# An output projection's loads moved three chunks ahead, and four stored columns turned into four stored rows

## The chip, the cores and the metric

The kernel runs on one core of a Trainium2 chip, as a single launch. The metric is the device time of one execution in microseconds. Engines are named as the profile does: PE is TensorE's matmul and PEld its weight loads, DVE is VectorE, ACT is ScalarE, POOL is GpSimd, and SP is the engine from which most DMAs are issued. A letter q behind an engine (SPq, ACTq) means its sequencer, which issues DMAs.

## The reference

One encoder layer on x of 2048 tokens by 1024 columns, float32. One input projection feeds two groups of heads: gated linear attention (four heads, result `o_a`, 512 columns) and multi-head latent attention (four heads, dense softmax over all 2048 keys, result `o_b`, 512 columns). Both are gated, joined, projected and normalized:

```python
o_a = gla_branch(g_q, g_k, g_v, g_gate, g_lr_f, g_lr_b, ...)
o_b = mla_branch(m_cq, m_ckv, m_kr, m_gate, positions, ...)   # p = softmax(s); o = (p @ v) * silu(gate)
mixed = jnp.concatenate([o_a, o_b], axis=-1) @ w_out
x = layer_norm(DEEPNORM_ALPHA * x + mixed, ln_g, ln_b)
```

The change lies in the last line but one and the last: the output projection with its residual and normalization, and in the softmax's denominators of the last attention block, which that projection reads.

## The kernel before

**Precision.** Every large product is made of three: an operand is split into a high and a low part (`hi`, a ScalarE copy, L336; `lo`, a subtraction on GpSimd or VectorE, L342), and `mm3` (L368 to L370) adds high x high, high x low and low x high.

**Stages.** Two sweeps over the tokens make the projections and the linear attention (to about 670 us in the profile). Then latent attention runs 16 blocks, each one head by 512 queries, with an order of all engines that is written out by hand as places in time (`PLACE`, `PLACE_LAST`, `PLACE_OUT`). Block i = 4b + h covers head h of the 512 tokens b. For each block the unnormalized output, 128 rows by 512 tokens, goes to the DRAM scratch `ob_s[b]` (`yc`, L1428), and the reciprocals of the softmax's sums go to `r_s[b]` (`keep`, L1406). The sums of a block are transposed and reduced into `rc`, a tile of 128 partitions by 4 (`tsum`, `rcp`): token e*128 + p stands in partition p, column e. So `keep` writes 4-byte elements, issued from ScalarE's queue: for blocks 0 to 14 one DMA of all four columns, for the last block one column at a time, after chunks 6, 7, 8 and 9 of the output projection.

**The output projection** (`OutProj`) works on 16 chunks of 128 tokens. Per chunk c:

- `load(c)` (L1589): four DMAs of 256 KB each on SP: `of<-oa_s` (linear attention's part), `gr<-gm_s` (the gate), `gr<-r_s` (the reciprocals, spread over 128 partitions) and `of<-ob_s` (latent attention's part). The tile `of` has two buffers in turn, and from chunk 4 on so has `gr`.
- `split(c)` (L1515): `oh` of the first half on ScalarE, `ol` of it on GpSimd, two multiplications of the second half by gate and reciprocals on GpSimd (L1609), then `oh` and `ol` of the second half.
- `load_res(c)` (L1619): 512 KB of x on SP into `xr`, three buffers.
- `product(c)` (L1640): two column halves of 24 matmuls each on TensorE. Odd chunks put both into a PSUM pair `po`; even chunks use the single banks `pmb` and `px`.
- `residual(c)` (L1651): `rr` = alpha * `xr` + product and its statistics on VectorE. `rr` has three buffers, so that of chunk c is that of chunk c−3, whose store must have landed.
- `finish(c)` (L1660): `u` from the statistics, `Ln` and `Exp` on ScalarE (L381, L382), the rest of the normalization on VectorE (L387 to L390, L1669, L1672), and two stores `out_dram<-rr` on SP (L1673). In the text, ln(c) means its two ScalarE instructions and out(c) its two stores.

Chunks 0 to 3 are woven into the end of the attention's order (`first`). From there on (L1506) the order of ScalarE, GpSimd and SP alone is held to the program's (`LATE_ORDER`), while TensorE and VectorE are ordered by the framework. Each of these queues works strictly in its order. Before the loop the program has load(4), the residual loads of 2 and 3, load(5), finish(0) and finish(1), split(4), the residual load of 4, and residual and finish of 2 and 3. Then, for each c from 4:

```python
with fixed():
    load(c + 2)
    split(c + 1)
    if c + 1 < NCH:
        op.load_res(rest[c + 1])
    op.product(rest[c])
    op.finish(rest[c])
with self.after(*last.values()), fixed():
    for f in {4: (tot, oh, ol), 5: (tsum, rcp), 7: (y, yc)}.get(c, ()):
        f(nb - 1)
    if 6 <= c < 10:
        keep(nb - 1, c - 6)
```

So on SP load(c+2) stands behind out(c−1). Chunks 12 to 15 read `r_s[3]` and `ob_s[3]`, to which the last block's results go in this loop.

Of the kernel before, what the change touches and what calls it, by code (L numbers as in the profile page):

```python
# [9 lines left out]
F32 = mybir.dt.float32  # L10
F32R = mybir.dt.float32r
I32 = mybir.dt.int32
AF = mybir.ActivationFunctionType
# [5 lines left out]
P = 128  # L19
# [8 lines left out]
QB = 512  # L28
# [36 lines left out]
    tot=11.2,  # L65
    tsum=12.04,
    rcp=13.55,
    keep=14.21,
    oh=12.34,
    ol=12.99,  # L70
    y=16.55,
    yc=16.9,
# [255 lines left out]
class K:  # L328
# [380 lines left out]
    def store(self, c):  # L709


        return self.nc.gpsimd if c in STORE_POOL else self.nc.sync
# [546 lines left out]
    def attention(self):  # L1259
        tc, nc = self.tc, self.nc  # L1260
        mm = nc.tensor.matmul
        V, G, Ac = nc.vector, nc.gpsimd, nc.scalar
        NP = NKT // 2
        with ExitStack() as ctx:
            qp = self.wz
            sp = ctx.enter_context(tc.tile_pool(name="sp", bufs=NP + 4, reuse_waits="tile"))
            bp = ctx.enter_context(tc.tile_pool(name="bp", bufs=2, reuse_waits="tile"))
            bank = lambda n, bufs=1: ctx.enter_context(tc.tile_pool(name=n, bufs=bufs, space=PSUM, reuse_waits="tile"))
            pM, pO, pX, pA, pS = bank("pM"), bank("pO"), bank("pX"), bank("pA"), bank("pS", 2)
            blocks = [(h, b) for b in range(NQB) for h in range(H)]  # L1270
            nb = len(blocks)
            stt = [dict(s=[None] * NP) for _ in blocks]
# [130 lines left out]
                V.reciprocal(rc, rc)  # L1403
                d["rc"] = rc

            def keep(i, e=None):  # L1406
                h, b = blocks[i]
                es = slice(0, 4) if e is None else slice(e, e + 1)
                Ac.dma_start(self.r_s[b][:, h].rearrange("o (e p) -> p (o e)", p=P)[:, es], stt[i]["rc"][:, es])

            def oh(i):
                d = stt[i]
# [30 lines left out]
            op = OutProj(self, ctx, qp, bp, sp, pS, pM, pX)  # L1443
# [8 lines left out]
            def at(f, i, j=None):  # L1452
                p = PLACE_LAST.get(f, PLACE[f]) if i == nb - 1 else PLACE[f]
                return p[j] if isinstance(p, tuple) else p

            own = (("tot", tot), ("tsum", tsum), ("rcp", rcp), ("keep", keep), ("oh", oh), ("ol", ol), ("y", y), ("yc", yc))
            for i in range(nb):
                for j in range(NP):
                    t = NP * i + j
# [48 lines left out]
            rest = {c: o for c, o in enumerate(first)}  # L1508

            def load(c):  # L1510
                if c < NCH:
                    rest[c] = dict(c=c)
                    op.load(rest[c])

            def split(c):  # L1515
                if c < NCH:
                    op.hi(rest[c], 0)
                    op.lo(rest[c], 0)
                    op.gate(rest[c])
                    op.hi(rest[c], 1)  # L1520
                    op.lo(rest[c], 1)

            with fixed():
                load(4)
                for c in (2, 3):
                    op.load_res(rest[c])
                load(5)
                for c in (0, 1):
                    op.finish(rest[c])
                split(4)  # L1530
                op.load_res(rest[4])
                for c in (2, 3):
                    op.residual(rest[c], 0)
                    op.residual(rest[c], 1)
                    op.finish(rest[c])
            for c in range(4, NCH):
                with fixed():
                    load(c + 2)
                    split(c + 1)
                    if c + 1 < NCH:  # L1540
                        op.load_res(rest[c + 1])
                    op.product(rest[c])
                    op.finish(rest[c])
                with self.after(*last.values()), fixed():
                    for f in {4: (tot, oh, ol), 5: (tsum, rcp), 7: (y, yc)}.get(c, ()):
                        f(nb - 1)
                    if 6 <= c < 10:
                        keep(nb - 1, c - 6)


class OutProj:
# [190 lines left out]
```

## Time and profile before

| | |
|---|---|
| three runs | 1363.34, 1357.39 and 1355.76 us, median 1357.39 |
| the profiled execution | 1363.85 us |
| its span | 1362.1 us, 1.75 of the execution lie around it |

Windows of the profiled execution, in us from the start of its span:

| stretch | what runs | PE busy | granted PE clock | DMA share |
|---|---|---|---|---|
| 0 to 600 | projections, linear attention | 572.84 of 600 | 0.99 | 0.41 |
| 600 to 700 | their end, start of attention | 97.17 of 100 | 1.00 | 0.47 |
| 700 to 1140 | attention blocks | 439.36 of 440 | 1.00 | 0.18 |
| 1140 to 1193.23 | last block, output chunks 0 to 2 among it | 51.42 of 53.23 | 1.00 | 0.38 |
| 1193.23 to 1352.35 | output chunks 3 to 15 | 149.17 of 159.12 | 0.97 | 0.67 |
| 1352.35 to 1362.1 | last residual, normalization, store | 0.14 of 9.75 | 0.61 | 0.14 |

How to read the rows that follow. A row of a timeline has the start in us, the duration, the engine, the line of the kernel, the operation, the tiles it writes and reads, the shapes, and in brackets the engine's idle time before it with what ended it. Where several of one kind follow each other they are one row with their count, and the duration runs from the first's start to the last's end. A row of windows has, for each engine, the busy time and the number of instructions, then the clock granted to TensorE as a share of full speed, the mean busy share of the 16 DMA engines and the GB/s they moved. A row of DMA issues ends with the median us from issue to landing.

### The profile page before, as it was taken

The page shows a single profiled execution, that of the slowest core. Times are in us where ns is not written, and L with a number is a line of the kernel's source. Part 1 is how long each engine was busy: PE and PEld are TensorE (multiplying, and loading weights), DVE is VectorE, ACT ScalarE, POOL GpSimd, SP SyncE. Part 2 cuts the span into 40 slices and gives each one's busy share as a digit, 9 for nine tenths or more (in the row PEclk, how much of TensorE's full clock was granted, in tenths as well). Part 3 has the DMA queues.
Part 4 walks back from the last instruction along what each step waited for, and adds up shares of the span by engine and source line. Part 5 has one row for each costly group of instructions (what it writes and reads, how often), then busy time and mean ns, then how long its engine had stood idle before and what let it go on. Part 6 is the DMA issues. An engine that isn't in the chain of part 4 may idle for free.

```text
span 1362.1 us, 20027 instructions
## 1 busy us (share of the span) xinstructions
PE 1310.1 (96%) x7120; PEld 1142.6 (84%) x7120; DVE 937.3 (69%) x1683; ACT 814.6 (60%) x1338; POOL 807.5 (59%) x509
## 2 busy tenths in 40 slices
PE   6899999999989999999999999999999999999987
PEld 6789898989979999999788888888888887777775
DVE  7747755454684444455788888888888888397576
ACT  6555555645565555665687878878888887311110
POOL 2542323232357666663198888889999998734352
PEclk9999999999999999999999999999999999999988
DMA  7322222313283566654601111121133110467863
GB/s 250 85 63 79 62 78 74 90 51 89 78 284 132 184 203 196 200 186 148 177 1 39 40 39 39 40 63 55 55 85 86 43 35 27 115 203 177 184 177 116
DMA packets 108836, 147.39 MB, mean 108 GB/s; under 512 B 17886, under 2 KB 63326, under 8 KB 108736
## 3 DMA queue, kind: packets, MB, share of 16 engines
q1 hardware_dynamic: 99408, 143.46, 35.6%
q0 software_dynamic: 832, 2.62, 0.5%
q8 instruction: 56, 0.92, 0.3%
q10 hardware_dynamic: 8496, 0.03, 0.3%
q14 instruction: 44, 0.36, 0.1%
HBM read 94.93 MB, written 51.15 MB: 107 GB/s over the span
## 4 chain that ended last, share of the span: by engine, by line
PE 60%; DVE 4%; DMA 3%; POOL 2%; issue 1%; ACT 1%; SPq 0%; DVEq 0%; POOLq 0%; ACTq 0%
PE pS L1293 4%; PE pS L1296 4%; PE pS L1295 4%; PE pS L1297 4%; PE pS L1294 4%; PE o L368 4%; PE o L369 4%; PE o L370 4%; PE pz L368 2%; PE pz L369 2%; PE pz L370 2%; PE ipm L368 2%; PE ipm L370 2%; PE ipm L369 2%; PE po L370 1%; PE po L369 1%
## 5 line engine op out<-in xcount | busy, mean ns | idle before, releaser
L342 POOL TENSOR_TENSOR pl<-s,ph 128x1024 fp32r<-128x1024 f32 x128 | 307.1, 2416 | 67.2 <-ACT ph L336 61.8
L1315 DVE TENSOR_TENSOR rm<-pS,rm 128x512 f32<-128x512 f32 x210 | 144.8, 690 | 44.6 <-ACT s L1302 39.5
L1302 ACT ACTIVATE s<-pS 128x1024 f32<-128x1024 f32 x128 | 131.4, 1027 | 68.1 <-PE pS L1297 66.7
L1339 DVE TENSOR_TENSOR s<-s,mb 128x1024 f32<-128x1024 f32 x128 | 151.2, 1213 | 9.1 <-PE mb L1333 9.0
L336 ACT ACTIVATE ph<-s 128x1024 fp32r<-128x1024 f32 x128 | 135.1, 1057 | 16.7 <-PE o L370 16.1
L1343 ACT ACTIVATE s<-s 128x1024 f32<-128x1024 f32 x128 | 131.4, 1050 | 13.4 <-DVE s L1339 13.3
L368 PE MATMUL ipa<-wah,xah 128*128 128x384 f32 (+1 forms) x384 | 131.1, 341 | 6.7 <-ACT wah L336 6.7
L838 POOL TENSOR_TENSOR Us<-Us,cw 128x512 f32<-128x512 f32 x16 | 18.2, 1139 | 200.7 <-DVE Us L835 171.3
L370 PE MATMUL ipa<-wah,xal 128*128 128x384 f32 (+1 forms) x384 | 126.0, 328 | 0.0
L369 PE MATMUL ipa<-wal,xah 128*128 128x384 f32 (+1 forms) x384 | 125.5, 327 | 0.0
L1293 PE MATMUL pS<-qh,ckvT_h 128*128 128x512 f32 x256 | 103.7, 405 | 0.7 <-ACT s L1343 0.4
L368 PE MATMUL o<-ph,vh 128*128 128x512 f32 x256 | 102.6, 401 | 0.0
L370 PE MATMUL o<-ph,vl 128*128 128x512 f32 x256 | 101.3, 396 | 0.0
L1296 PE MATMUL pS<-rh,krs 128*128 128x512 f32 x256 | 101.2, 395 | 0.0
L369 PE MATMUL o<-pl,vh 128*128 128x512 f32 x256 | 101.1, 395 | 0.0
L1295 PE MATMUL pS<-qh,ckvT_l 128*128 128x512 f32 x256 | 100.8, 394 | 0.0
L1297 PE MATMUL pS<-rl,krs 128*128 128x512 f32 x256 | 100.7, 393 | 0.0
L1294 PE MATMUL pS<-ql,ckvT_h 128*128 128x512 f32 x256 | 100.6, 393 | 0.0
L1366 DVE TENSOR_TENSOR ap<-ap,s 128x512 f32<-128x512 f32 x120 | 83.1, 692 | 7.5 <-ACT s L1343 5.6
L342 POOL TENSOR_TENSOR ol<-of,oh 128x512 fp32r<-128x512 f32 x32 | 43.4, 1356 | 71.6 <-ACT oh L336 71.6
L368 PEld LDWEIGHTS ipa<-wah,xah 128*128 128x128 f32 x384 | 74.2, 193 | 7.2 <-ACT wah L336 6.7
L368 PE MATMUL pz<-xch,wzh 128*128 128x256 f32 x256 | 75.1, 294 | 0.0
(316 smaller groups left out, 3904.9 us busy)
## 6 DMA issues: line engine op xcount, KB each, us to landing
xcf<-xT_dram SPq DMA_DIRECT2D x16, 512.0 KB, 4.2
xr<-x_dram SPq DMA_DIRECT2D x16, 512.0 KB, 6.9
out_dram<-rr SPq DMA_DIRECT2D x32, 256.0 KB, 2.4
xaf<-xT_dram SPq DMA_DIRECT2D x14, 512.0 KB, 4.3
qdb<-qd_s SPq DMA_DIRECT2D x16, 256.0 KB, 4.7
SU<-su_s SPq DMA_DIRECT2D x16, 256.0 KB, 4.7
oib<-oi_s SPq DMA_DIRECT2D x16, 256.0 KB, 4.7
ub<-u_s SPq DMA_DIRECT2D x16, 256.0 KB, 3.8
```

Source lines behind the costliest of these rows:

```text
L336: return nc.scalar.activation(dst, src, AF.Copy).ins
L342: return e.tensor_tensor(dst, src, hi.bitcast(F32), ALU.subtract).ins
L368: mm(out, ah, bh, start=start, stop=False)
L369: mm(out, ah, bl, start=False, stop=False)
L370: mm(out, al, bh, start=False, stop=stop)
L1293: mm(ps[:, e], kh, qh, start=True, stop=False)
L1294: mm(ps[:, e], kh, ql, start=False, stop=False)
L1295: mm(ps[:, e], kl, qh, start=False, stop=False)
L1296: mm(ps[:, e], kr, rh, start=False, stop=False)
L1297: mm(ps[:, e], kr, rl, start=False, stop=True)
L1315: V.tensor_tensor(d["rm"], src[:, e], d["rm"], ALU.max)
L1339: V.tensor_tensor(s, s, d["mb"][:, None, :].to_broadcast([P, 2, QB]), ALU.subtract)
```

## The change

- `keep` stores all four columns again, and only blocks 0 to 14 use it.
- For the last block, after chunk 6, `turn` transposes `rc` on TensorE into the PSUM tile `rt` (128x4 to 4x128) and copies it with ScalarE into `rr15`, four partitions of 128; `store` writes it from SP to `r_s[3]` as four rows of 512 bytes. The four column stores after chunks 6 to 9 go.
- Before the loop, split(4), a new load(6) and the residual load of 4 come ahead of finish(0) and finish(1).
- In the loop, load(c+3) stands behind split(c+1), in place of load(c+2) ahead of it.

```diff
-            def keep(i, e=None):
+            def keep(i):
                 h, b = blocks[i]
-                es = slice(0, 4) if e is None else slice(e, e + 1)
-                Ac.dma_start(self.r_s[b][:, h].rearrange("o (e p) -> p (o e)", p=P)[:, es], stt[i]["rc"][:, es])
+                Ac.dma_start(self.r_s[b][:, h].rearrange("o (e p) -> p (o e)", p=P), stt[i]["rc"])
+
+            def turn(i):
+
+                d = stt[i]
+                t = pA.tile([P, QB], F32, tag="ap", name=f"rt{i}")
+                nc.tensor.transpose(t[0:4, 0:P], d["rc"], self.ident)
+                d["rr"] = bp.tile([4, P], F32, tag="ofl", name=f"rr{i}", bufs=1)
+                Ac.activation(d["rr"], t[0:4, 0:P], AF.Copy)
+
+            def store(i):
+                h, b = blocks[i]
+                nc.sync.dma_start(self.r_s[b][:, h].rearrange("o (e p) -> (o e) p", p=P), stt[i]["rr"])
...
                 load(5)
+                split(4)
+                load(6)
+                op.load_res(rest[4])
                 for c in (0, 1):
                     op.finish(rest[c])
-                split(4)
-                op.load_res(rest[4])
...
             for c in range(4, NCH):
                 with fixed():
-                    load(c + 2)
                     split(c + 1)
+                    load(c + 3)
...
-                    for f in {4: (tot, oh, ol), 5: (tsum, rcp), 7: (y, yc)}.get(c, ()):
+                    for f in {4: (tot, oh, ol), 5: (tsum, rcp), 6: (turn, store), 7: (y, yc)}.get(c, ()):
                         f(nb - 1)
-                    if 6 <= c < 10:
-                        keep(nb - 1, c - 6)
```

## The prediction

> **What bounds the kernel now.** I began with the page, then cut the last stage at the starts of its chunks, then asked which waits stood in the cuts.
>
> ```profile
> span 1362.1 us, 20027 instructions
> PE 1310.1 (96%) x7120; PEld 1142.6 (84%) x7120; DVE 937.3 (69%) x1683; ACT 814.6 (60%) x1338; POOL 807.5 (59%) x509
> ```
>
> TensorE is the bound, so a change that moves no matmul can only win TensorE's idle or half-clocked time. Windows laid along the output product, one per chunk of 48 matmuls (chunks 4, 5, 6, 7, 10, 11 and 14; columns: length, busy time of each engine, granted clock, DMA share, GB/s):
>
> ```profile
> 1204.16:1215.07 10.91, 10.91 (x50) 8.88 (x48) 10.88 (x24) 1.97 (x6) 2.21 (x3) 1.00 0.51 179
> 1215.07:1228.97 13.90, 11.83 (x50) 8.78 (x49) 12.91 (x21) 2.15 (x5) 6.77 (x5) 1.00 0.47 138
> 1229.32:1244.58 15.26, 12.93 (x52) 10.00 (x50) 12.18 (x18) 2.19 (x5) 9.05 (x7) 0.89 0.53 175
> 1244.58:1255.46 10.88, 10.88 (x50) 9.01 (x48) 5.82 (x12) 1.67 (x4) 5.16 (x4) 1.00 1.00 199
> 1277.95:1290.25 12.30, 11.35 (x50) 8.85 (x49) 10.40 (x17) 1.67 (x4) 4.87 (x4) 1.00 0.69 187
> 1290.25:1308.81 18.56, 13.96 (x50) 10.54 (x49) 10.53 (x14) 2.19 (x5) 9.01 (x7) 0.82 0.60 139
> 1330.57:1341.45 10.88, 10.88 (x50) 9.01 (x49) 10.48 (x15) 1.56 (x4) 5.22 (x4) 1.00 0.43 140
> ```
>
> An undisturbed chunk takes 10.88. Over that, chunk 5 loses 3.0, chunk 6 4.4, chunk 10 1.4 and chunk 11 7.7: 16.5 in all. Chunks 12 to 15 lose nothing with loads two ahead. So the change is judged on four chunks.
>
> Chunk 11 waited for ScalarE's second high part, and that for a load; the first row is TensorE's, the second from the chain of waits, then ScalarE's stores of reciprocals (three of four), then the landings of residual inputs `xr` in this stage:
>
> ```profile
> 1297.60 0.79 PE L368 MATMUL po<-woh,oh 128*128 128x512 f32 x1 [4.47 <-ACT oh L336]
> 1283.38 10.76 DMA of<-ob_s
> 1246.90 0.34 ACTq L1409 DMA_DIRECT2D r_s<-rc  x1
> 1259.16 0.34 ACTq L1409 DMA_DIRECT2D r_s<-rc  x1
> 1284.33 0.33 ACTq L1409 DMA_DIRECT2D r_s<-rc  x1
> DMA to landing us min/median/max: 6.0/6.9/17.9
> ```
>
> Bandwidth around these stores (same columns as above):
>
> ```profile
> 1244.00:1252.00 8.00, 8.00 (x37) 6.64 (x36) 6.02 (x13) 1.04 (x3) 2.52 (x2) 1.00 0.79 260
> 1252.00:1259.00 7.00, 7.00 (x32) 5.74 (x32) 3.27 (x7) 0.99 (x4) 2.66 (x3) 1.00 1.11 59
> 1264.00:1271.00 7.00, 7.00 (x33) 5.79 (x32) 0.00 (x0) 0.63 (x1) 3.55 (x3) 1.00 1.14 80
> 1271.00:1276.00 5.00, 5.00 (x24) 4.14 (x23) 4.27 (x9) 1.00 (x3) 0.00 (x0) 1.00 1.12 310
> 1289.00:1296.00 7.00, 4.13 (x19) 3.08 (x17) 0.20 (x1) 0.00 (x0) 1.65 (x2) 1.00 0.75 119
> ```
>
> Some 5 us after each of these stores of 128 elements of 4 bytes, the DMA engines are as busy as ever and move 59, 80, 119 GB/s in place of 260 to 310, for 7 us. The 17.9 is `xr` of chunk 8, caught by two such jams; it made chunk 8's normalization, and so chunk 10's split, late (1.4). Chunk 11's load was caught by the last jam (7.7). So 9.1 of the 16.5 hangs on how the last block's reciprocals are stored.
>
> Chunk 6 has another cause:
>
> ```profile
> 1212.59 9.38 SPq L1673 DMA_DIRECT2D out_dram<-rr  x4
> 1222.06 0.38 SPq L1600 DMA_DIRECT2D of<-oa_s  x1
> 1230.66 2.64 POOL L1609 TENSOR_TENSOR of<-of,gr 128x512 f32<-128x512 f32 x2 [2.92 <-DMA of<-ob_s]
> ```
>
> Its load stood on SP behind the stores of chunks 2 and 3, though its buffer was free since 1207.1 (`ol` of chunk 4, below).
>
> **The change, part by part.** *Row store.* The four jams go: −1.4 −7.7 = −9.1. Added are one transpose, one ScalarE copy of 4x128 and one 2 KB store. No row shows them; the nearest are the transposes `sx`, 0.27 each, and ScalarE's 0.20 (one element a lane) and 0.62 (512 a lane). The copy is in ScalarE's slack behind chunk 6. The transpose is on TensorE's path: 0.1 to 0.3, I take 0.1. The store has until chunk 12's load, three chunks later. Four ScalarE issues (0.34) leave a queue that is idle there.
>
> *Loads in the loop.* load(c+3) now waits on SP for GpSimd's end of split(c+1) instead of VectorE's out(c−1). Behind it on SP stand `xr` of c+1 and out(c). For the odd chunk 7, ended at 1255.46, ScalarE's normalization came 3.4 later:
>
> ```profile
> 1258.61 0.20 ACT L381 ACTIVATE ln_l<-u 128x1 f32<-128x1 f32 x1 [4.49 <-DVE u L1667]
> ```
>
> So, from the end T of product c−1, split(c+1) begins at T+3.5 and takes 6.7 (rows below): it ends near T+10.2. Four load issues take 2.3; `xr` lands 6.9 after its own: T+19.4, ahead of the end of product c+1 at T+21.8. out(c) is due near T+17, with SP free since T+13; who waits for it is the residual of chunk c+3, at T+43. Nothing new is on the path; were the 2.4 of cover for `xr` gone, each us more would cost one. The gain is chunk 6's 4.4; chunks 12 to 15 show that there is no more.
>
> *The start, split(4) and load(6) ahead of finish(0) and finish(1).* ScalarE, GpSimd and SP keep program order here, VectorE's order is rebuilt. Moved ahead are two ScalarE and four GpSimd instructions and, on SP, four load issues (2.3) and one of `xr` (0.6). Rows of ScalarE (ln of chunk 0, `oh` halves of 4, `oh` of 5), GpSimd (gate of 4, `ol` of 4, `ol` of 5) and VectorE (rr of 2 and 3, u of 3), and landings of the loads issued 1191 to 1195:
>
> ```profile
> 1192.87 0.20 ACT L381 ACTIVATE ln_l<-u 128x1 f32<-128x1 f32 x1 [4.01 <-DVE u L1667]
> 1199.92 0.61 ACT L336 ACTIVATE oh<-of 128x512 fp32r<-128x512 f32 x1
> 1204.69 0.63 ACT L336 ACTIVATE oh<-of 128x512 fp32r<-128x512 f32 x1 [4.16 <-POOL of L1609]
> 1214.34 0.62 ACT L336 ACTIVATE oh<-of 128x512 fp32r<-128x512 f32 x1
> 1201.98 2.67 POOL L1609 TENSOR_TENSOR of<-of,gr 128x512 f32<-128x512 f32 x2
> 1205.40 1.68 POOL L342 TENSOR_TENSOR ol<-of,oh 128x512 fp32r<-128x512 f32 x1 [0.74 <-ACT oh L336]
> 1219.79 1.27 POOL L342 TENSOR_TENSOR ol<-of,oh 128x512 fp32r<-128x512 f32 x1 [0.74 <-ACT oh L336]
> 1201.96 0.68 DVE L1657 SCALAR_TENSOR_TENSOR rr<-xr,pmb 128x512 f32<-128x512 f32 x1
> 1209.24 0.68 DVE L1657 SCALAR_TENSOR_TENSOR rr<-xr,po 128x512 f32<-128x512 f32 x1
> 1213.82 0.14 DVE L1667 TENSOR_SCALAR u<-mv 128x1 f32<-128x1 f32 x1
> of<-ob_s SPq DMA_DIRECT2D x1, 256.0 KB, 7.4
> 1226.62 2.03 SPq L1673 DMA_DIRECT2D out_dram<-rr  x2
> DMA to landing us min/median/max: 4.7/5.3/5.8
> ```
>
> Chunk 4's last load, issued at 1192.9, lands at 1200.3. Gate 2.7, `oh` 0.7, `ol` 1.3: split(4) ends at 1205.1, 2.0 earlier. But ln(0) and ln(1) now stand behind its second `oh`: 1203.7 in place of 1192.9. VectorE does rr of chunk 2 at 1201.7, then waits for ln(0), and goes on at 1205.1. Ahead of rr(3) now stand thirteen operations of 512 columns at 0.62 to 0.7 and some small ones: 1214.0 in place of 1209.2. And rr(3) takes the buffer of rr(0), so out(0) must have landed. out(0) now follows load(6) and `xr` of 4 on SP. In the old order such a group began at 1222.06 and the stores behind it (last two rows) landed at 1232.4 and 1233.0, 10.4 and 11.0 after. From 1205.1 that is 1215.5 to 1216.1; I take 1215.6. Then six more operations to u(3), 1219.5, and chunk 5's split starts at 1220.0 in place of 1214.3: **+5.7**, straight onto chunk 5, whose TensorE waits are on that split. Bounds: +4.1 if out(0) lands in time (1214.0 holds), +9.0 if it lands as late as the slowest store in the chain of waits:
>
> ```profile
> 1261.35 10.20 DMA out_dram<-rr
> ```
>
> (issued at 1208.8, landing at 1219.0). Chunk 6's split then has its load early, starts after ln(4) near 1228 and ends by 1236; its product starts at 1235. It needs the second half 2.8 later, so its 4.4 is gone whatever chunk 5 does.
>
> The 5.7 us wait ahead of chunk 5 may bring the clock down, as here (the stretches after chunk 6's and chunk 11's waits):
>
> ```profile
> 1234.97:1238.38 3.41, 3.01 (x7) 2.43 (x8) 3.38 (x7) 0.93 (x3) 2.43 (x3) 0.50 0.51 191
> 1296.41:1303.24 6.83, 5.51 (x12) 3.92 (x13) 6.59 (x12) 1.55 (x4) 4.88 (x5) 0.50 0.65 184
> ```
>
> Half a clock for 3.4 us costs 1.7. But the first twelve matmuls of chunk 5 wait for its second half anyway (6.7 us from the start of the split, 1214.34, to its end, 1221.06), and run inside that wait. I take 0.3, bounds 0 and 1.7. The Trainium skill, "TensorE: Matmul & The Clock Gate", Part 1, says that an idle window of some 3.4 us halves the clock until a busy one has passed; by it the full 1.7 would come, a total of −6.0. The rows agree on the size and are shorter on the cause: 1.71 of waiting was enough at chunk 6.
>
> Sum: −9.1 −4.4 +5.7 +0.3 +0.1 = **−7.4**. The profiled execution took 1363.85 (span 1362.1); with the change 1356.4. The runs shown are 1363.34, 1357.39 and 1355.76, so the profile is at their slow end. Taken off the median of 1357.39: **1350.0**.
>
> **Rivals.**
> 1. *The median run never lost the jams.* Whether chunk 11's load beats the last jam is close: the slow stretch is there at 1289, and a load issued at 1283.38 that took the 6.0 of the quickest `xr` would land at 1289.4. The profile lies 6.5 above the median, near the 7.7. Then the change saves the median run only −4.4 +6.1 −1.4: +0.3, **1357.7**. Against it: the early stages have waits of their own that could make the spread.
> 2. *Slower: the start costs more than chunk 6 gives back.* ln(0) behind split(4) is the mechanism. With out(0) at 1219.0, the clock at 1.7, and no jam losses in the median run: −4.4 +9.0 +1.7 +0.1 = +6.4, **1363.8**. It decides as soon as chunk 5's split starts more than 4.4 after 1214.3 and the jams are no loss. For it: VectorE was busy 10.88 of 10.91 through chunk 4, so it has nothing to absorb a stall with.
> 3. *The row store jams too*, or the jam is not the store's: chunks 10 and 11 keep 9.1, and the sum is +1.7, **1359.1**. Against it: the slow stretches follow three of the four stores. By the Trainium skill, "DMA: Bandwidth & Descriptors", Specifications, transfers under 512 B are read-modify-write; rows of 512 B would be just clear of it. No row here shows such a store.
> 4. *out(0) lands in time and nothing is lost to the clock*: −9.1 −4.4 +4.1 +0.1 = −9.3, **1348.1**.
>
> **How the numbers follow.** The forecast, 1350.0, with its own range 1348 to 1353, holds 0.42; rival 1 0.22, rival 2 0.18, rival 3 0.07, rival 4 0.09, and 0.02 is for what I overlooked. The range 1346 to 1361 leaves out rival 2 and that rest: 2 in 10. A change under 0.5% (6.8 us, about what a measurement of this kernel can tell from none) ends at 1350.6 and 1364.2. Faster: rival 4 and 0.30 of the forecast, 0.39. Slower: two thirds of rival 2, where the landing or the clock costs more than its bounds here, and the rest, 0.14. Same: what is left, 0.47.
>
> **What would show it.** Right: no stretch under 200 GB/s with a DMA share near 1 between chunks 7 and 12; chunks 6 to 15 at 10.9 each; chunk 5 near 19.6 with its first wait on ScalarE's `oh`; ln(0) on ScalarE after chunk 4's second `oh`; rr of chunk 3 waiting for a store `out_dram<-rr`. Wrong: chunk 5 at 14 or less (the start costs nothing), slow stretches that remain, or waits on `xr` in the loop.

## The result, and the profile after

| | runs | median us | lowest and highest |
|---|---|---|---|
| before | 22 | 1357.20 | 1351.04 to 1363.34 |
| after | 22 | 1361.68 | 1357.74 to 1363.75 |

The ratio is 1.003, with a 95% interval of 1.0019 to 1.0041: 4.5 us slower, where 7.4 us faster was forecast. The two profiled executions say the reverse: before took 1363.85, after 1359.89. So two questions are open: which of the steps failed, and why profile and median differ in sign.

The first lines of after's page:

```profile
span 1358.1 us, 20026 instructions
PE 1308.9 (96%) x7121; PEld 1142.0 (84%) x7121; DVE 950.6 (70%) x1683; ACT 813.7 (60%) x1339; POOL 805.7 (59%) x509
```

TensorE is still the bound, and again what counts is its idle time in the output chunks. Windows of after, one for each of chunks 5, 6, 7, 8 and 11 (columns as before: length, then busy time of PE, PEld, DVE, ACT and POOL, granted clock, DMA share, GB/s); chunk 8's begins with `y`, the last block's three matmuls, which take 0.7:

```profile
1215.13:1234.00 18.87, 13.88 (x50) 10.39 (x50) 18.07 (x29) 3.60 (x9) 10.17 (x8) 0.82 0.39 133
1234.35:1245.33 10.98, 10.98 (x51) 8.99 (x50) 8.79 (x15) 1.36 (x4) 4.08 (x4) 1.00 0.60 192
1245.36:1256.24 10.88, 10.88 (x50) 9.01 (x49) 8.31 (x16) 0.57 (x3) 1.30 (x1) 1.00 0.69 228
1256.24:1272.05 15.81, 12.89 (x53) 9.35 (x52) 11.75 (x14) 3.35 (x8) 10.89 (x8) 1.00 0.42 115
1293.81:1304.69 10.88, 10.88 (x49) 9.01 (x48) 10.60 (x15) 1.56 (x4) 5.37 (x5) 1.00 0.65 198
```

Chunk 6's 4.4 is gone and so is chunk 11's 7.7; chunk 5 has grown from 13.90 to 18.87, as the prediction had it (+5.0 for +5.7). Chunk 8 is new: with `y` it needs 11.7 undisturbed (10.9 and 0.7 in before) and took 15.8, 4.1 more. The prediction had chunks 6 to 15 at 10.9 each and no cost at chunk 8.

The slow stretches behind the column stores are gone, too. Windows of after over the times of four rows that the prediction shows of before (slow there at 1252, 1264 and 1289, fast at 1271):

```profile
1252.00:1259.00 7.00, 5.97 (x25) 4.26 (x24) 4.28 (x9) 0.79 (x2) 1.10 (x1) 1.00 0.55 197
1264.00:1271.00 7.00, 6.81 (x30) 5.63 (x31) 4.86 (x6) 0.74 (x2) 5.61 (x5) 1.00 0.76 185
1271.00:1276.00 5.00, 5.00 (x24) 4.14 (x23) 2.66 (x5) 0.00 (x0) 0.00 (x0) 1.00 1.02 330
1289.00:1296.00 7.00, 7.00 (x32) 5.79 (x32) 6.83 (x9) 0.63 (x1) 4.17 (x4) 1.00 0.53 186
```

At shares of 0.53 to 0.76 the DMA engines move 185 to 197 GB/s and at 1.02 they move 330; in before's slow stretches they moved 59 to 119 at shares of 0.75 to 1.14.

ScalarE's timeline in after, at the start and around chunk 8:

```profile
1202.39 0.63 ACT L336 ACTIVATE oh<-of 128x512 fp32r<-128x512 f32 x1 [6.42 <-POOL of L1619]
1202.93 0.18 ACT L381 ACTIVATE ln_l<-u 128x1 f32<-128x1 f32 x1
...
1219.34 0.61 ACT L336 ACTIVATE oh<-of 128x512 fp32r<-128x512 f32 x1
...
1250.80 0.20 ACT L382 ACTIVATE ln_y<-ln_l 128x1 f32<-128x1 f32 x1
1257.04 0.27 ACT L1416 ACTIVATE rr<-rt 4x128 f32<-4x128 f32 x1 [6.04 <-PE y L369]
1257.22 0.61 ACT L336 ACTIVATE oh<-of 128x512 fp32r<-128x512 f32 x1
```

At the start ln(0) stands right behind chunk 4's second `oh`, and chunk 5's split begins at 1219.34 (forecast 1220.0). At chunk 8 the new copy `rr<-rt` stands idle for 6.04 before it runs. Its input `rt` was there since 1245.6, when the transpose between chunks 6 and 7 ended. What ended the wait is `y`, which runs after chunk 7. Behind the copy, in program order, stands the first `oh` of chunk 8. By ScalarE alone it could have run at 1251.0; it ran at 1257.2, and TensorE had to wait for both halves of split(8).

Why should a copy of `rt` wait for `y`? `turn` gives `rr15` the tag `ofl` with one buffer. That is the buffer of `ofl15`, the low part of the last block's output, and `y` reads it. By this the copy may not write before `y` has read. The first two experiments test it.

### The profile page after: what moved, and what is told of

Same layout as the page of the kernel before. It is cut to its first block, busy times and chain, and to the rows that moved or that the text cites. A ratio compares the mean times of both kernels' runs of the same rounds, so it can differ in the third digit from the quotient of the medians.

```text
span 1358.1 us, 20026 instructions
## 1 busy us (share of the span) xinstructions
PE 1308.9 (96%) x7121; PEld 1142.0 (84%) x7121; DVE 950.6 (70%) x1683; ACT 813.7 (60%) x1339; POOL 805.7 (59%) x509
## 4 chain that ended last, share of the span: by engine, by line
PE 46%; issue 4%; POOL 2%; DMA 1%; DVE 1%; ACT 1%; SPq 0%; DVEq 0%; POOLq 0%; ACTq 0%
PE pS L1293 4%; PE pS L1296 4%; PE pS L1295 4%; PE pS L1297 4%; PE pS L1294 4%; PE o L368 4%; PE o L369 4%; PE o L370 4%; PE po L369 1%; PE po L370 1%; PE po L368 1%; POOL of L1619 1%; PE pmb L370 1%; PE pmb L369 1%; DMA of<-oa_s 1%
## 5 line engine op out<-in xcount | busy, mean ns | idle before, releaser
L1315 DVE TENSOR_TENSOR rm<-pS,rm 128x512 f32<-128x512 f32 x210 | 144.9, 690 | 44.5 <-ACT s L1302 39.4
L369 PEld LDWEIGHTS ipa<-wal,xah 128*128 128x128 f32 x384 | 74.0, 193 | 1.3 <-DVE wal L342 0.6
```

Source lines behind the costliest of these rows:

```text
L369: mm(out, ah, bl, start=False, stop=False)
L1315: V.tensor_tensor(d["rm"], src[:, e], d["rm"], ALU.max)
```

## The experiments

All executions lose their time in a few chunks, so one table serves them all. It gives, for each profile, the end of chunk 4, the time lost over the undisturbed 10.88 in chunks 5, 6, 8 (with `y`, over 11.7) and 10 to 12 together, and the stretch from the end of chunk 4 to the end of the span. Without any loss that stretch is about 130.7 (before: 147.0 − 16.5 = 130.5; after: 143.0 − 8.0 − 0.1 − 4.1 = 130.8). Chunks from 7 on that are not listed lose under 0.3.

| kernel, execution us | end of 4 | 5 | 6 | 8 | 10 to 12 | stretch |
|---|---|---|---|---|---|---|
| before, 1363.85 | 1215.1 | 3.0 | 4.4 | 0 | 9.1 | 147.0 |
| before_again, 1369.23 | 1218.3 | 3.1 | 4.6 | 0 | 11.0 | 149.2 |
| before_look2, 1358.81 | 1217.1 | 3.0 | 1.9 | 0 | 4.5 | 139.9 |
| before_look3, 1364.46 | 1217.9 | 3.0 | 4.5 | 0 | 6.7 | 144.7 |
| before_look4, 1365.65 | 1219.0 | 3.0 | 4.8 | 0 | 6.6 | 144.9 |
| before_look5, 1360.88 | 1218.1 | 3.1 | 4.3 | 0 | 3.1 | 141.0 |
| before_look6, 1364.50 | 1218.4 | 3.1 | 4.8 | 0 | 5.6 | 144.3 |
| after, 1359.89 | 1215.1 | 8.0 | 0.1 | 4.1 | 0 | 143.0 |
| after_again, 1362.24 | 1216.9 | 8.6 | 0.1 | 4.0 | 0 | 143.6 |
| after_look3, 1362.33 | 1215.9 | 9.7 | 0.1 | 4.0 | 0 | 144.6 |
| own_buffer, 1359.12 | 1215.7 | 10.7 | 0.1 | 0 | 0 | 141.6 |
| row_alone, 1356.92 | 1219.0 | 2.9 | 2.4 | 0 | 0 | 136.1 |
| row_shared, 1360.90 | 1215.0 | 3.1 | 6.1 | 4.1 | 0 | 144.1 |
| loads_alone, 1366.36 | 1217.2 | 8.8 | 0.1 | 6.8 | 1.2 | 147.4 |
| finish_first, 1354.83 | 1218.8 | 2.8 | 0.7 | 0 | 0 | 134.3 |
| stores_first, 1356.20 | 1217.7 | 5.1 | 0.7 | 0 | 0 | 136.7 |
| split5_early, 1350.93 | 1217.1 | 0 | 1.2 | 0 | 0 | 132.1 |

The times that follow were measured later, on three chips. There before took medians of 1363.0 to 1365.0, where the first pair had 1357.2, so kernels are compared by their ratio to before on the same chip and in the same set of runs.

### A buffer of its own for the copy, and the reverse

own_buffer is the changed kernel with

```diff
-                d["rr"] = bp.tile([4, P], F32, tag="ofl", name=f"rr{i}", bufs=1)
+                d["rr"] = bp.tile([4, P], F32, tag="rr", name=f"rr{i}", bufs=1)
```

> The changed kernel with one edit: rr15 gets a buffer of its own (tag rr) in place of ofl's. Theory W (the copy waits for y because it reuses the buffer that y reads, and split(8) stands behind it on ScalarE): the copy runs at about 1246, right after rt; the first oh of chunk 8 at about 1251 in place of 1257.2; chunk 8 takes 10.9 in place of 14.2 and starts 0.6 sooner; 4.0 less than the changed kernel, about 1357.7. Rival (the copy waits for y by the order of the queues, or chunk 8's split is late for another reason, such as its load): the copy still ends its wait with y, chunk 8 keeps its 14.2, about 1361.7. In both, chunk 5 keeps 18.8 with its wait of 4.7.

row_shared is the row store alone, in the order of before, with the buffer shared as in the changed kernel (row_alone, below, has it with a buffer of its own):

```diff
-                d["rr"] = bp.tile([4, P], F32, tag="rr", name=f"rr{i}", bufs=1)
+                d["rr"] = bp.tile([4, P], F32, tag="ofl", name=f"rr{i}", bufs=1)
```

> row_alone with one edit, the reverse of own_buffer's: rr15 shares ofl's buffer, as in the changed kernel. Theory W: the copy waits for y here too, with loads and start as in the kernel before; chunk 8 takes about 14 in place of 10.9 and the stretch from the end of chunk 4 to the end of the span 140 in place of 136.1. Rival (the wait bites only where the loads stand behind the splits): chunk 8 keeps 10.9.

ScalarE's timeline in own_buffer, then the window of `y` and chunk 8 there, then the same two of row_shared:

```profile
1252.82 0.20 ACT L382 ACTIVATE ln_y<-ln_l 128x1 f32<-128x1 f32 x1
1252.93 0.25 ACT L1416 ACTIVATE rr<-rt 4x128 f32<-4x128 f32 x1
1253.09 0.61 ACT L336 ACTIVATE oh<-of 128x512 fp32r<-128x512 f32 x1
```

```profile
1259.53:1271.27 11.74, 11.74 (x53) 9.66 (x52) 10.43 (x16) 2.04 (x5) 5.98 (x5) 1.00 0.71 232
```

```profile
1258.02 0.27 ACT L1416 ACTIVATE rr<-rt 4x128 f32<-4x128 f32 x1 [9.19 <-PE y L369]
1258.19 0.61 ACT L336 ACTIVATE oh<-of 128x512 fp32r<-128x512 f32 x1
```

```profile
1257.35:1273.05 15.70, 12.78 (x53) 9.26 (x52) 13.04 (x16) 3.35 (x8) 10.88 (x8) 1.00 0.51 162
```

With a buffer of its own the copy has no wait: it starts 0.1 behind the second instruction of ln(6), which stands ahead of it on ScalarE (so not right behind `rt`, as I had expected), 6.7 ahead of `y` (near 1259.7), and split(8) starts 0.16 behind it. Chunk 8 loses nothing. With the shared buffer in the old order the copy waits 9.19 for `y`, and chunk 8 loses its 4.1 again. So the wait is the buffer's, whatever the order of the loads, and costs 4.0 to 4.1 in four profiles out of four. The time of own_buffer itself was 1359.65 against 1364.98 for before (ratio 0.9963, 0.995 to 0.9976); row_shared took 1363.87 against 1363.74 (0.9994, 0.9974 to 1.0014). Two expectations missed in other chunks. In own_buffer's profile chunk 5 lost 10.7, and not 8.0; why is seen below. In row_shared's, chunk 6 lost 6.1, and the stretch came to 144.1 in place of 140; chunk 6 runs ahead of the copy, and why it lost so much there stays open.

### The row store alone, and the loads alone

row_alone is before with `turn` and `store` (own buffer) in place of the four column stores, loads and start untouched:

```diff
-                    for f in {4: (tot, oh, ol), 5: (tsum, rcp), 7: (y, yc)}.get(c, ()):
+                    for f in {4: (tot, oh, ol), 5: (tsum, rcp), 6: (turn, store), 7: (y, yc)}.get(c, ()):
                         f(nb - 1)
-                    if 6 <= c < 10:
-                        keep(nb - 1, c - 6)
```

> The kernel before with the row store alone (turn and store after chunk 6, rr15 in a buffer of its own), loads and start as before. Theory J (a median run of before loses little to the column stores: its 1357.2 leaves 2.5 for them after the 3.0 of chunk 5 and the 4.4 of chunk 6): 0 to 2.5 below the kernel before, about 1355. Rival, my forecast's first term (every run loses 9.1): about 1348. In both, no stretch under 200 GB/s with a DMA share near 1 behind chunk 7, and chunks 10 and 11 at 10.9.

loads_alone is the opposite: the start and the loop of the changed kernel, and the four column stores of before. Against before its loop reads:

```diff
-                    load(c + 2)
                     split(c + 1)
+                    load(c + 3)
```

> The kernel before with the loads and the start of the changed kernel, and the four column stores kept. By my terms corrected by the trace of after: chunk 5 +5.0, chunk 6 -4.4, chunk 8 undisturbed by the copy. If loads three ahead also cover the slow stretches behind the column stores, chunks 10 and 11 come to 10.9: +0.6 less up to 2.5 against before, 1355 to 1358. Rival (the slow stretches still bite, at another chunk, because a store of 128 small elements delays whatever load is then under way): a stall of 3 to 8 remains between chunks 8 and 12, 1360 to 1366.

Windows of row_alone: chunks 10 and 11, then a stretch behind the row store in which the DMA engines are busy:

```profile
1279.96:1290.84 10.88, 10.88 (x49) 9.01 (x48) 10.47 (x15) 1.56 (x4) 5.45 (x5) 1.00 0.32 104
1290.84:1301.72 10.88, 10.88 (x49) 9.01 (x48) 7.20 (x14) 1.67 (x4) 3.90 (x4) 1.00 0.79 260
...
1266.00:1273.00 7.00, 7.00 (x33) 5.79 (x32) 5.83 (x10) 1.56 (x4) 2.46 (x3) 1.00 0.69 224
```

The slow stretches and the losses in chunks 10 to 12 go with the column stores, and with nothing else changed. The ratio to before was 0.9949 (0.9932 to 0.9965), or 1357.26 against 1364.98: −7.7. That is well over the 2.5 that I had left for it, and near my first 9.1. Not all of it need be the store's: chunk 6, ahead of these stores, lost 2.4 in this profile, and 4.3 to 4.8 in six of the seven of before. The Trainium skill, "DMA: Bandwidth & Descriptors", Specifications, has transfers under 512 B as read-modify-write; rows of exactly 512 B, one store of four, show no slow stretch here, which agrees.

The row store differs from the column stores in three ways: it is one DMA in place of four, it is made of longer pieces, and it comes from SP and not from ScalarE's queue. The first alone is not it. Block 14's `keep`, the same in both kernels, is a single DMA of 512 elements; in after it is issued at 1154.85 and lands 9.1 later, and windows ahead of that landing and behind it read:

```profile
1161.00:1163.00 2.00, 2.00 (x10) 1.65 (x9) 1.86 (x3) 1.67 (x2) 2.00 (x2) 1.00 1.04 33
1165.00:1167.00 2.00, 2.00 (x11) 1.60 (x9) 0.66 (x1) 0.00 (x0) 0.00 (x0) 1.00 0.56 178
```

Pieces and queue are not told apart by any run here, and that read-modify-write is what slows the rest is not shown either.

loads_alone took 1366.86 against 1364.98 (ratio 1.0022, 1.0007 to 1.0036). Its rows: a slow stretch of its DMA in windows, `xr` of chunk 7 in a view of that tile, ScalarE's and TensorE's timelines, and the window of `y` and chunk 8:

```profile
1262.00:1267.00 5.00, 3.38 (x15) 2.45 (x14) 1.04 (x2) 0.00 (x0) 0.00 (x0) 1.00 0.93 69
```

```profile
DMA to landing us min/median/max: 12.8/12.8/12.8
```

```profile
1268.91 0.20 ACT L381 ACTIVATE ln_l<-u 128x1 f32<-128x1 f32 x1 [9.13 <-DVE u L1668]
...
1269.25 0.58 ACT L1431 ACTIVATE yc<-y 128x512 f32<-128x512 f32 x1
```

```profile
1269.88 0.80 PE L368 MATMUL px<-woh,oh 128*128 128x512 f32 x1 [4.50 <-ACT yc L1431]
```

```profile
1258.90:1277.48 18.58, 14.08 (x54) 11.10 (x52) 11.06 (x17) 2.67 (x6) 6.92 (x6) 0.82 0.75 146
```

The expectation's rival was that a slow stretch delays whatever load is under way, and so it does; that loads three ahead cover the stretches fails. Where TensorE lost time, in chunks 8 and 11, no split waited for its own load; but `xr` of chunk 7, issued at 1253.0, took 12.8 to land. The residual of chunk 7 began at 1265.96, 6.9 after its product; its normalization came late on ScalarE, behind it in program order stood `yc`, which empties the bank that chunk 8's second half needs, and TensorE waited 4.5 for `yc`. Chunk 11 lost its 1.2 to another `xr`: that of chunk 9 took 13.9 to land, its normalization came late, and split(11) stood behind it on ScalarE. So loading further ahead didn't take the column stores' loss away; it moved it.

### The start: what chunk 5 waits for

The changed kernel's start costs chunk 5 its 8.0 to 9.7. VectorE's timeline at rr of chunk 3, first in own_buffer, then in after_look3:

```profile
1217.97 1.28 DVE L1667 SCALAR_TENSOR_TENSOR rr<-xr,po 128x512 f32<-128x512 f32 x2 [3.38 <-DMA out_dram<-rr]
```

```profile
1217.17 1.28 DVE L1667 SCALAR_TENSOR_TENSOR rr<-xr,po 128x512 f32<-128x512 f32 x2 [2.51 <-DMA out_dram<-rr]
```

It waits for a store, out(0), as forecast. In after itself the row names another releaser:

```profile
1215.11 1.28 DVE L1667 SCALAR_TENSOR_TENSOR rr<-xr,po 128x512 f32<-128x512 f32 x2 [2.23 <-PE px L369]
```

But rr of chunk 3 doesn't read `px`, and the second store of out(0), issued at 1208.1, landed 6.8 later, at 1214.9: rr begins 0.2 behind that landing, as in own_buffer (issued at 1209.8, 8.0, landed at 1217.8). That rr waited for the store here too is inferred from this. What the store's landing moves, chunk 5 pays: rr of chunk 3 began at the end of chunk 4 in after, 0.6 behind it in after_again, 1.3 in after_look3 and 2.3 in own_buffer, and chunk 5 lost 8.0, 8.6, 9.7 and 10.7.

Two edits of own_buffer take the mechanism apart. stores_first leaves split(4) ahead of both finishes, but puts the finishes ahead of load(6):

```diff
                 split(4)
-                load(6)
-                op.load_res(rest[4])
                 for c in (0, 1):
                     op.finish(rest[c])
+                load(6)
+                op.load_res(rest[4])
```

> own_buffer with one edit: finish(0) and finish(1) between split(4) and load(6), so that ln(0) still stands behind split(4) on ScalarE, but out(0) no longer behind load(6) on SP. If the landing of out(0) is what held rr of chunk 3 (it had to wait 3.4 for it in own_buffer), it has no wait now, and chunk 5's wait for its split falls from 7.0 to about 3.5. If ln(0) behind split(4) is the cost by itself, the wait stays at 5 to 7.

finish_first puts finish(0) and finish(1) ahead of split(4) and load(6) (as in own_buffer, rr15 has its own buffer):

```diff
+                for c in (0, 1):
+                    op.finish(rest[c])
                 split(4)
                 load(6)
                 op.load_res(rest[4])
-                for c in (0, 1):
-                    op.finish(rest[c])
```

> own_buffer with one edit: finish(0) and finish(1) again ahead of split(4), load(6) behind split(4), and so ahead of out(2) and out(3) but behind out(0). Theory: out(0) then lands before VectorE comes to rr of chunk 3, chunk 5 is back at about 13.9 and chunk 6 at 10.9; the end of chunk 4 to the end of the span takes 133.5 in place of 141.5, about 8 less than own_buffer and 2.5 less than row_alone. Rival (load(6) ahead of out(2) and out(3) costs in another place what it gives at chunk 6): chunks 5 and 6 together lose 5.3 or more, as in row_alone.

Windows of stores_first (TensorE's wait ahead of chunk 5, chunk 5 itself) and of finish_first (chunks 5 and 6):

```profile
1217.89:1219.77 1.88, 0.00 (x0) 0.00 (x0) 1.84 (x5) 0.93 (x3) 0.00 (x0) 1.00 0.62 142
1219.77:1233.74 13.97, 13.20 (x48) 10.08 (x49) 13.59 (x21) 2.04 (x5) 7.87 (x7) 0.88 0.68 227
```

```profile
1218.79:1232.44 13.65, 11.75 (x50) 8.73 (x48) 13.34 (x20) 2.15 (x6) 8.76 (x7) 1.00 0.59 189
1232.79:1244.35 11.56, 11.29 (x52) 8.92 (x50) 9.29 (x17) 1.32 (x5) 5.55 (x4) 1.00 0.61 193
```

Of own_buffer's 10.7 in chunk 5, 5.6 go when out(0) no longer follows load(6) on SP (the wait ahead of the chunk falls from 7.0 to 1.9, further than the 3.5 expected), 2.3 more when ln(0) no longer follows split(4) on ScalarE, and 2.8 were there before. These are differences of single profiles, and own_buffer's 10.7 is the largest of five with this start; against after's 8.0 the first is 2.9. In finish_first load(6) is early all the same, and chunk 6 loses only 0.7. It came to 0.9921 of before (0.9908 to 0.9935), stores_first to 0.9920 (0.9903 to 0.9937); the profiles differ by 2.4 in the stretch, the times don't tell the two apart.

### A version that beats both

split5_early is finish_first with split(5) moved ahead of the residual of chunk 3; in the loop they are then left out for c = 4:

```diff
                     op.finish(rest[c])
+                    if c == 2:
+                        split(5)
+                        load(7)
+                        op.load_res(rest[5])
```

> finish_first with one edit: split(5), load(7) and the residual load of 5 between finish(2) and the residual of chunk 3, where they stood behind finish(3). If chunk 5's loss of 3.0 in the kernel before is only its split standing behind ln(3) on ScalarE, chunk 5 comes to about 11 and the stretch from the end of chunk 4 to the end of the span to 130.6, 3 less than finish_first. Rival (VectorE, which is busy all through chunk 4, or out(3) behind load(7), makes chunk 6 or 7 late by as much): the same as finish_first.

Its windows for chunks 5 and 6:

```profile
1217.10:1227.99 10.89, 10.89 (x50) 8.96 (x49) 10.58 (x24) 1.82 (x6) 2.19 (x3) 1.00 0.73 253
1228.34:1240.44 12.10, 11.28 (x51) 8.91 (x50) 11.93 (x18) 2.19 (x5) 7.32 (x6) 1.00 0.52 177
```

Chunk 5 has no loss left, chunk 6 1.2. The stretch is 132.1, 2.2 less than in finish_first and not 3, since chunk 6 lost 0.5 more. The time is 1350.70 against 1364.96 for before and 1364.87 for the changed kernel on the same chip: 0.9885 of before (0.9872 to 0.9899).

### Before and after again

> The kernel before, unedited, for a second profile. Theory J: chunk 11 loses much less than 7.7 here, since whether its load beats the last slow stretch is a matter of a microsecond; the span is 4 to 8 below 1362.1 by that alone. Rival: chunk 11 loses 7.7 again, and the spread of the times comes from stages ahead of chunk 3, which then ends at another time than 1204.2.

> The changed kernel, unedited, on one chip with the next three. Theory W: chunk 8 loses 4 again behind the copy that waits for y; chunk 5 loses 8 or more behind out(0). On a chip where the kernel before loses 8 to 11 to the slow stretches in most runs, it should come out 0 to 4 faster than before; where before loses them seldom, slower, as first measured. Rival: it is slower than before by the same 0.3% on every chip.

> The kernel before, unedited, one of three more profiles. If the column stores' loss is what spreads its times (1351 to 1369 over all chips), the stretch from the end of chunk 4 to the end of the span varies between about 138 and 149, and the loss sits in chunks 8 to 12; the rest is the start of chunk 3, at 1193 to 1197. Rival: that stretch is 147 to 149 every time, and only what lies ahead of chunk 3 spreads.

> The kernel before, unedited, second of three more profiles; the two theories expect what they expect of before_look2: a stretch from the end of chunk 4 that varies from profile to profile, or one of 147 to 149 each time.

> The kernel before, unedited, third of three more profiles; the two theories expect what they expect of before_look2: a stretch from the end of chunk 4 that varies from profile to profile, or one of 147 to 149 each time.

> The kernel before, unedited, once more, for an execution near the 1357 of the first measurement's median. So far the losses in chunks 10 to 12 were 4.5 to 11.0 and in chunk 6 1.9 to 4.8, and the two moved with the time. Theory: an execution at 1357 or below has 4.5 or less in chunks 10 to 12 and about 2 in chunk 6. Rival: it has the same 7 to 11 and an early start of chunk 3 (1193 or before).

> The kernel before, unedited, with the same two expectations as before_look5: at a time of 1357 or below 4.5 or less in chunks 10 to 12, or else 7 to 11 there and an early start of chunk 3.

> The changed kernel, unedited, beside before_look5 and before_look6 on the same chip. Theory: the stretch from the end of chunk 4 to the end of the span is 143 to 146, with 8 to 11 lost in chunk 5, 4 in chunk 8 and nothing elsewhere; the ratio to before is above 1 only where before's runs lie near 1357. Rival: some other stage of the changed kernel is slower and adds the rest.

On two chips the changed kernel took 1.0002 of before (0.9986 to 1.0017) and 0.9999 (0.9978 to 1.0019): no difference, where the first pair had 0.3%. So the rival of the same 0.3% everywhere is not borne out, though on one of the two chips the intervals meet. In after_again and after_look3 chunks 5 and 8 lose what was expected, and no other stage loses more than 0.1. The two extremes among the profiles of before, by windows: chunks 6, 10, 11 and 12 of before_look2, and chunks 10, 11 and 12 of before_again:

```profile
1231.37:1244.10 12.73, 11.57 (x51) 8.94 (x50) 11.23 (x18) 2.19 (x5) 9.46 (x7) 1.00 0.62 204
1277.48:1289.16 11.68, 11.17 (x49) 8.93 (x48) 5.80 (x13) 1.67 (x4) 4.29 (x4) 1.00 1.12 146
1289.16:1302.36 13.20, 11.46 (x50) 8.85 (x48) 8.38 (x16) 1.67 (x4) 5.79 (x5) 1.00 0.76 174
1302.36:1314.60 12.24, 11.47 (x49) 8.86 (x48) 11.15 (x15) 2.19 (x5) 9.16 (x7) 1.00 0.57 189
```

```profile
1281.42:1293.61 12.19, 11.45 (x50) 8.85 (x48) 7.40 (x15) 1.67 (x4) 4.87 (x5) 1.00 0.98 169
1293.61:1306.64 13.03, 11.63 (x49) 8.67 (x48) 4.38 (x9) 1.67 (x4) 3.73 (x3) 1.00 1.21 106
1306.64:1325.05 18.41, 14.71 (x49) 10.94 (x49) 13.30 (x22) 2.19 (x5) 11.20 (x8) 0.81 0.74 226
```

The column stores cost before something in each of seven profiles, from 3.1 to 11.0, with a middle value of 6.6; which chunk pays differs from one execution to the next. Chunk 6 varies too, 1.9 to 4.8. The stretch went from 139.9 to 149.2, so the rival of 147 to 149 each time fails. The expectation of before_again, that chunk 11 would lose much less, held for that chunk (2.2) but not for the loss, which had gone to chunk 12 (7.5). The end of chunk 4 spreads from 1215.1 to 1219.0 besides. No execution at 1357 or below was caught, so the expectation of before_look5 for such a one was not met by a case; the two nearest to it, at 1358.8 and 1360.9, have the two smallest losses in chunks 10 to 12, 4.5 and 3.1.

## Why the prediction was wrong

The prediction's steps, in its order:

- *The row store takes the jams away*: right. row_alone and after have no slow stretch and no loss in chunks 10 to 12, and loads_alone, which keeps the column stores, has both. Rival 3 falls. The size, 9.1, is that of one execution; over seven profiles it is 3.1 to 11.0, and in six of them chunk 12 pays too, which the prediction had as losing nothing.
- *Chunk 6's 4.4 goes*: right, 0.1 is left (the four `sx` aside). Its size in before is 1.9 to 4.8.
- *The start costs +5.7 in chunk 5*: right in mechanism, +5.0 in after's profile, +5.6 and +6.7 in two more, +7.7 in own_buffer; all within the bounds +4.1 and +9.0. The lower bound, +4.1 with out(0) landing in time, was too high: in stores_first rr of chunk 3 has no wait, and chunk 5 lost 2.1 over before.
- *The transpose on TensorE's path, 0.1*: it took 0.03 (`rt` at 1245.33, chunk 7 at 1245.36).
- *The clock, 0.3*: nothing in after, where split(5) started 5.0 later and chunk 5 took 5.0 longer.
- *"The copy is in ScalarE's slack behind chunk 6"*: **this step failed.** I priced the copy by its duration and looked at when ScalarE had time, and not at when its output buffer came free. The diff shows `tag="ofl"` and `bufs=1`; `ol` and `yc` have the same tag; `y`, which reads that buffer, runs after chunk 7. The copy therefore had to wait until 1257, and on an engine in program order split(8) waits with it. Cost: 4.1.
- *"Taken off the median of 1357.39"*: **this step failed as well.** I sized the gain on an execution that I had seen to be at the slow end (its 1363.85 is above all 22 runs of before, 1351.04 to 1363.34), and took it off the median of three runs. Its −9.1 is more than five of the other six profiles of before had to lose.

The sum with the copy in it, made against the profile's own time, is −9.1 − 4.4 + 5.0 + 4.1 + 0.0 = −4.4, and the two profiled executions differ by −4.0. So, execution against execution, the copy was the one term that was missing. For the medians the gain is smaller. With the middle values of the seven profiles of before, 6.6 and 4.5, and chunk 5 at +5.0 to +6.7, the sum is −2.0 to −0.3, and two chips show none (1.0002 and 0.9999). With the two profiles that lost least, 4.5 and 1.9 in one and 3.1 and 4.3 in the other, it is +1.7 to +4.4, against the first pair's +4.5. That before lost so little in the first pair's median run is inferred from its time: no profile of such a run was taken, and this part of the 4.5 stays open.

Rival 1 had this mechanism for the median run, in too strong a form: the seven profiles differ in what the column stores cost, but none loses nothing to them. It left the copy out as well. Rival 2, the start outweighing the rest, gave 1363.8 from +9.0 in chunk 5 and +1.7 in the clock. Both were smaller in after (+5.0 and nothing), and without the copy's 4.1 the two profiles that lost least would have left −2.4 to +0.3. That its 1363.8 lies near the 1361.68 measured is chance. What row_alone, finish_first and split5_early show is that the change holds two gains (the row store, and load(6) ahead of out(2)), and that it gave them back at two places: ahead of chunk 5 and at chunk 8.

## What to carry to other kernels

A new small instruction is priced by what it waits for as much as by its duration: look up who else uses its output's buffer and when the last reader runs, and then who stands behind it on its engine. When a wait is only a matter of which load is under way, take several profiles before putting a number on it, and make the sum and its subtraction with the same execution. Moving loads further ahead didn't remove what slowed them here; it changed who was caught.

## What was not expected of the hardware

The granted clock fell to half behind some of TensorE's waits and not behind others of about the same length. Windows of after: the wait ahead of chunk 5 in two parts, then the matmuls behind it, until the clock was back:

```profile
1215.29:1218.40 3.11, 0.00 (x0) 0.00 (x0) 3.11 (x7) 0.00 (x0) 0.00 (x0) 1.00 0.39 150
1218.40:1220.01 1.61, 0.00 (x1) 0.01 (x1) 1.61 (x4) 0.93 (x3) 0.00 (x0) 0.50 0.00 0
1220.01:1225.20 5.19, 4.92 (x11) 3.43 (x12) 5.16 (x10) 0.63 (x1) 4.35 (x4) 0.50 0.00 0
1225.20:1227.00 1.80, 1.80 (x9) 1.26 (x8) 1.80 (x3) 0.27 (x2) 0.86 (x1) 0.99 0.38 146
```

Chunk 12 of before_look3 (the longer of its two waits is 2.23, the other 0.63) and chunk 6 of before_look5 (1.41 and 0.62; its last row is the part at half clock):

```profile
1305.94:1320.26 14.32, 11.47 (x50) 8.86 (x49) 11.86 (x22) 1.65 (x5) 8.86 (x7) 1.00 0.69 220
```

```profile
1232.38:1247.57 15.19, 13.16 (x52) 10.08 (x51) 11.07 (x18) 2.19 (x5) 9.40 (x7) 0.89 0.62 205
1238.37:1241.75 3.38, 3.38 (x9) 2.60 (x9) 3.24 (x7) 0.60 (x2) 2.13 (x2) 0.50 0.51 193
```

The shorter wait brought the clock down, the longer didn't. The Trainium skill, "TensorE: Matmul & The Clock Gate", Part 1, has the halving after an idle window of some 3.4 us. In after the clock fell 3.1 into the wait of 4.72, which agrees roughly, and stayed at half for 6.8, twice that window; in before_look5 it stayed there for 3.4, but behind waits of 1.41 and 0.62, shorter than such a window. What decides which short wait brings the clock down, no run here shows.

In after the half clock cost nothing. It held the first twelve matmuls of chunk 5, which need only the first half of the split; the second half's `ol` ended at 1226.06, and the first matmul that reads it started at 1226.11.
